# A two-layer stream encoder on one core: 40 hidden chunks ahead of the second dense stage, and its gates in three passes of 4, 5 and 7 blocks

## The chip, the core and the metric

The kernel runs on one core of a Trainium2 chip. The metric is the device time of one execution in microseconds (us). Engine names are those of the profile: PE is TensorE, PEld its weight loads, DVE VectorE, ACT ScalarE, POOL GpSimd, SP SyncE. POOL and SP only issue DMAs here: POOL the gathers by index (q0), SP the rest (q1).

## What is computed

Two layers run over 512 new frames (four blocks B0 to B3 of 128 tokens) and a sample of 64 tokens (S). Each layer has a mixer (attention, mLSTM, chunk MLP) and then PEER, a layer of 16384 one-neuron experts of which each token uses 8 heads x 16:

```python
def block(xi):                       # peer(), shortened
    q = (xi @ w_q)...                # 8 heads, normalised
    s = jnp.einsum('thcd,hckd->thck', q, keys)
    ...                              # top 16 of 128 x 128 per head: experts e, softmax gates g
    act = jax.nn.gelu(jnp.einsum('thkd,td->thk', u_tab[e], xi), approximate=False)
    return jnp.einsum('thk,thkd->td', (g * act), v_tab[e])
x = x + peer(xn2, peer_wq, peer_keys, peer_u, peer_v)
```

u_tab and v_tab are 16384 x 1024 floats each. A final RMSNorm follows.

## The kernel before

PEER is done in two ways at the same time. For two of the four blocks (256 tokens; B2 and B3 in layer 1) it is **dense**: all 16384 experts are gone through in 128 chunks of 128 experts. The other tokens are **gathered**: for each of a token's pairs POOL fetches the row of u or v by index, one row for each of 128 tokens, 512 KB. DVE multiplies a u row with the normalised input and sums it (L984), and adds a v row, times its gated activation, to the token's x (L996). In layer 1 blocks B0 and B1 are gathered beside the dense stage: 128 u tiles, then 128 v tiles, for B0 and then for B1, 512 in all. The 64 pairs of S are done earlier.

The dense stage of a layer (`peer_dense`, `first_gate`, `gate_batch`) works so, chunk by chunk:
- A **lead** loads the U chunk (SP, 512 KB, two buffers) and PE makes the hidden values H of 256 tokens, 8 products of 256 columns (L1059, in the trace 16 entries, since a float32 product has two). ACT applies the gelu into a tile `pre` or `A` (L1068). The first 8 x PRE chunks go to `pre`, whole blocks of 8 chunks that take gate buffers; later ones go to single tiles `A`, LAG + 2 of them.
- DVE multiplies the hidden chunk with its gates (L1092), in place.
- The V chunk is loaded (SP, two buffers) and PE adds the chunk's **product** to the outputs y, 4 products of 512 columns (L1099, 8 entries).

The **gates** are a matrix of 256 tokens x 16384 experts, nearly all zero. It is built in 16 blocks W of 8 chunks. A **pass** builds the blocks of one span at once, in 32 **batches** of 8 tokens. In each batch DVE makes a one-hot `o2` of 1024 elements per partition (L1020), a one-hot `o1` whose width goes with the blocks of the span (L1022), and weights it (L1024, twice that width). PE multiplies them, 16 weight loads and 16 products as wide as 8 x the blocks (L1028), and ACT copies the result into each block (L1030). QB lists the blocks of each pass. Before, layer 1 has two passes of 8. The first pass (`first_gate`) stands ahead of chunk 0; the others stand among the chunks of the span before, in its last WIN chunks:

```python
left = ci - (nq - win) + 1
while more and left > 0 and done < min(32, left * 32 // (win - 1)):
    if not nxt:
        nxt = [self.gate_block(l, c // 8 - ci // 8 + nb + i) for i in range(QB[l][q + 1])]
    self.gate_batch(nxt, c - ci + nq, 8 * done, self.psum([8, 8 * len(nxt)]))
    done += 1
if nl < NCH and len(acts) <= lag:
    lead(nl)
```

So a lead is issued only while no more than LAG (8) hidden chunks are in hand: after 8 x PRE + LAG leads ahead, the first 8 x PRE chunks have none of their own. HOME gives each block's buffer: `0` one tile of its own, `a` one of GATE_A = 4, which `pre` shares, `b` one of GATE_B[1] = 5. A buffer is waited for until its last reader is done.

A scheduler orders each engine's instructions when the program is built; gathers have low priority and fill DVE's gaps, but once ordered, each engine keeps to its order. Gate products are tied behind the last gate batch issued (`behind`). The final norm of a token block (`final`) squares on ACT (L236) into one tile `y` that all share, so each waits for the output DMA of the one ahead.

Of the kernel before, what the change touches and what calls it, by code (L numbers as in the profile page):

```python
# [36 lines left out]
WT = 1056  # L37
TD = 256
NG = TD + NS
QB = [[8, 8], [8, 8]]  # L40
WIN = [[24], [16]]
GATE_A, GATE_B = 4, [6, 5]
HOME = ["0aaabbbbbba0aaab", "0aabbbbbaa0aabbb"]
MID = 10 ** 6
LOW = 10 ** 7
PS_TAG = {"p": "mm", "a": "mm", "r": "mm", "o": "o", "tp": "tr", "ta": "tr", "tr": "tr"}
# [2 lines left out]
T_BUFS = {"t": 4, "tr": 2}  # L49
DENSE_T = 4  # L50
LAG = [4, 8]
PRE = [1, 2]
EARLY_LEADS = 5
REST_STEP, REST_PARTS = 4, 16
ORDER = ["N1 P1 N2 Q1 M1+P2 O1+Q2 S1+M2 F1+O2 S2", "N1 P1 Q1 M1+R O1 S1 N2 P2 F1+Q2 M2 O2"]
# [65 lines left out]
class Build:  # L121
# [911 lines left out]
    def gate_block(self, l, b):  # L1033
        home = HOME[l][b]
        pool, tag = (self.ca, "W0") if home == "0" else (self.wb if home == "a" else self.wb2, "W")
        W = pool.tile([P, 8, TD], F32, tag=tag, name=tag)
        return W

    def first_gate(self, l):
        nb = QB[l][0]  # L1040
        self.W0 = [self.gate_block(l, i) for i in range(nb)]
        for t0 in range(0, TD, 8):
            self.gate_batch(self.W0, 0, t0, self.psum([8, 8 * nb]))
            if l == 0:
                self.gated = self.mark.ins
            yield

    def peer_dense(self, l, group, xT):
# [5 lines left out]
        def lead(c):  # L1054
            U = self.up.tile([P, KC, P], F32, tag="U", name="U")
            nc.sync.dma_start(U, h["uT"][l, c])
            hp = hh[:, c % 2]
            for k in range(KC):
                mm = nc.tensor.matmul(hp, U[:, k, :], xT[k], start=(k == 0), stop=(k == KC - 1))  # L1059
                if k == 0 and l and c < 8 * PRE[l] + lag:  # L1060
                    self.behind(mm, self.smark.ins)
            if c < 8 * PRE[l]:
                if c % 8 == 0:
                    pre.append(self.wb.tile([P, 8, TD], F32, tag="W", name="pre"))
                a = pre[-1][:, c % 8, :]
            else:
                a = self.da.tile([P, TD], F32, tag="A", name="A", bufs=lag + 2)
            nc.scalar.activation(a, hp, AF.Gelu)  # L1068
            acts.append(a)
        for c in range(8 * PRE[l] + lag):  # L1070
            lead(c)
# [3 lines left out]
        Ws = self.W0  # L1075
        for q, nb in enumerate(QB[l]):
            more = q + 1 < len(QB[l])
            nxt, done = [], 0
            nq = 8 * nb
            win = WIN[l][q] if more else 0  # L1080
            for ci in range(nq):
# [5 lines that stand above are left out]
# [30 lines left out]
    def run(self):  # L1117
# [9 lines left out]
        for l in range(DEPTH):  # L1127
# [20 lines left out]
            with ExitStack() as es:  # L1148
                self.dense_pools(es.enter_context, l)
                nlead = LAG[l] + 8 * PRE[l]  # L1150
                if l == 0:
# [115 lines left out]
```

## Time and profile before

| what | us |
|---|---|
| median of three runs | 3598.27 (3591.49 to 3602.72) |
| the profiled execution | 3593.99 |
| its span, first to last instruction | 3592.2 |
| PE busy in it | 3078.9 (86%) |
| DVE busy | 2568.6 (72%) |
| ACT busy | 669.8 (19%) |
| mean DMA rate | 295 GB/s |

Busy shares are means over stages with different limits; the table of stretches below is read by stage. Queues on one engine run in order, so an instruction that waits holds up all that stands behind it. "Chunk" below is always one of the 128 chunks of layer 1's dense stage.

### The profile page before, as it was taken

The page shows a single profiled execution, that of the slowest core. Times are in us where ns is not written, and L with a number is a line of the kernel's source. Part 1 is how long each engine was busy: PE and PEld are TensorE (multiplying, and loading weights), DVE is VectorE, ACT ScalarE, POOL GpSimd, SP SyncE. Part 2 cuts the span into 40 slices and gives each one's busy share as a digit, 9 for nine tenths or more (in the row PEclk, how much of TensorE's full clock was granted, in tenths as well). Part 3 has the DMA queues.
Part 4 walks back from the last instruction along what each step waited for, and adds up shares of the span by engine and source line. Part 5 has one row for each costly group of instructions (what it writes and reads, how often), then busy time and mean ns, then how long its engine had stood idle before and what let it go on. Part 6 is the DMA issues. An engine that isn't in the chain of part 4 may idle for free.

```text
span 3592.2 us, 41429 instructions
## 1 busy us (share of the span) xinstructions
PE 3078.9 (86%) x13384; PEld 2057.7 (57%) x13384; DVE 2568.6 (72%) x5915; ACT 669.8 (19%) x2589; POOL 1540.9 (43%) x1284
## 2 busy tenths in 40 slices
PE   8989877789999999996977896589636999999996
PEld 6767646646666666653543654267512666666663
DVE  4454777776787666667688898847997679666664
ACT  4444222400121000001221222122210012000000
POOL 0000000065545445547657335610777666565562
PEclk9999989889999999998978997699858999999998
DMA  5332322289999999999979687853989999999995
GB/s 182 101 98 82 95 91 86 80 327 409 386 341 392 409 407 398 409 409 376 352 225 349 237 317 276 287 192 114 339 290 380 409 386 358 404 397 393 407 400 214
DMA packets 299929, 1060.21 MB, mean 295 GB/s; under 512 B 36372, under 2 KB 39232, under 8 KB 299712
## 3 DMA queue, kind: packets, MB, share of 16 engines
q0 software_dynamic: 184320, 671.17, 49.7%
q1 hardware_dynamic: 115392, 386.38, 29.9%
q8 instruction: 107, 1.75, 0.2%
q14 instruction: 110, 0.90, 0.1%
HBM read 1048.09 MB, written 8.27 MB: 294 GB/s over the span
## 4 chain that ended last, share of the span: by engine, by line
PE 44%; DVE 17%; DMA 16%; issue 14%; POOL 7%; ACT 2%; SPq 0%; POOLq 0%; DVEq 0%; ACTq 0%
PE H L1059 12%; PE y L1099 11%; DMA row<-in_peer_v_dram,idx 10%; PE ps L396 7%; POOL row L960 7%; PE ps L407 6%; DVE row L984 4%; DMA row<-in_peer_u_dram,idx 3%; DVE x_b L996 2%; PE ps L216 1%; PE ps L1028 1%; PE ps L572 1%; PE ps L830 1%; PE ps L574 1%; DVE o L1020 1%
## 5 line engine op out<-in xcount | busy, mean ns | idle before, releaser
L960 POOL DMA_INDIRECT row<-in_peer_u_dram,idx x640 | 776.6, 1213 | 1456.4 <-DVE row L984 822.4
L960 POOL DMA_INDIRECT row<-in_peer_v_dram,idx x640 | 764.1, 1194 | 542.4 <-DVE x_b L996 277.6
L984 DVE SCALAR_TENSOR_TENSOR row<-row,xn 128x1024 f32<-128x1024 f32 x640 | 769.8, 1221 | 178.1 <-DMA row<-in_peer_u_dram,idx 169.0
L1099 PE MATMUL y<-V,A 128*128 128x512 f32 x1856 | 845.4, 604 | 32.2 <-DMA V<-in_peer_v_dram 32.0
L996 DVE SCALAR_TENSOR_TENSOR x_b<-row,hb,x_b 128x1024 f32<-128x1024 f32 x512 | 656.2, 1282 | 158.5 <-DMA row<-in_peer_v_dram,idx 150.0
L1099 PEld LDWEIGHTS y<-V,A 128*128 128x128 f32 x1856 | 356.2, 194 | 421.5 <-issue 398.5
L1059 PE MATMUL H<-xT,U 128*128 128x256 f32 x2048 | 475.3, 385 | 35.2 <-ACT A L1068 20.4
L1059 PE MATMUL H<-xTd,U 128*128 128x256 f32 x2048 | 468.5, 382 | 10.2 <-ACT A L1068 8.2
L1059 PEld LDWEIGHTS H<-xT,U 128*128 128x128 f32 x2048 | 384.5, 191 | 125.8 <-ACT A L1068 39.4
L1059 PEld LDWEIGHTS H<-xTd,U 128*128 128x128 f32 x2048 | 386.7, 191 | 103.9 <-issue 40.4
L407 PE MATMUL ps<-xT,w 128*128 128x320 f32 (+1 forms) x1280 | 336.4, 417 | 28.3 <-DMA w<-in_wt_dram 17.2
L1068 ACT ACTIVATE A<-H 128x256 f32<-128x256 f32 x232 | 88.9, 383 | 1346.2 <-PE H L1059 751.2
L407 PEld LDWEIGHTS ps<-xT,w 128*128 128x128 f32 x1280 | 244.3, 195 | 95.4 <-issue 13.3
L1092 DVE TENSOR_TENSOR A<-A,W 128x256 f32<-128x256 f32 x232 | 96.8, 422 | 217.5 <-ACT A L1068 209.6
L1030 ACT ACTIVATE W<-ps 128x64 f32<-128x64 f32 x1024 | 137.8, 321 | 295.7 <-PE ps L1028 202.7
L1028 PE MATMUL ps<-o,o 128*128 128x64 f16 x2048 | 85.9, 199 | 119.6 <-DVE o L1024 119.6
L996 DVE SCALAR_TENSOR_TENSOR x_s<-row,hb,x_s 128x1024 f32<-128x1024 f32 x128 | 164.1, 1282 | 32.9 <-DMA row<-in_peer_v_dram,idx 31.1
L1028 PEld LDWEIGHTS <-o 128*128 128x128 f16 x2048 | 79.9, 102 | 151.5 <-DVE o L1024 75.4
L1099 PE MATMUL y<-V,pre 128*128 128x512 f32 x192 | 105.0, 704 | 38.9 <-DMA V<-in_peer_v_dram 31.1
L396 PE MATMUL ps<-w,xT 128*128 128x512 f32 (+3 forms) x320 | 128.9, 554 | 5.7 <-DMA w<-in_wn_dram 5.7
L351 DVE TENSOR_TENSOR wl<-w,wh 128x1024 fp32r<-128x1024 f32 (+1 forms) x56 | 64.4, 1150 | 75.9 <-PE ps L396 56.0
L396 PE MATMUL ps<-w,mix 128*128 128x512 f32 (+1 forms) x224 | 110.9, 648 | 5.8 <-DMA w<-in_wn_dram 4.2
(314 smaller groups left out, 3004.6 us busy)
## 6 DMA issues: line engine op xcount, KB each, us to landing
V<-in_peer_v_dram SPq DMA_DIRECT2D x256, 512.0 KB
U<-in_uT_dram SPq DMA_DIRECT2D x256, 512.0 KB
w<-in_wt_dram SPq DMA_DIRECT2D x96, 512.0 KB
w<-in_wn_dram SPq DMA_DIRECT2D x80, 512.0 KB
row<-in_peer_u_dram,idx POOLq DMA_INDIRECT x640
row<-in_peer_v_dram,idx POOLq DMA_INDIRECT x640
w<-in_keysT_dram SPq DMA_DIRECT2D x16, 256.0 KB
w<-in_wn_dram SPq DMA_DIRECT2D x8, 264.0 KB
```

Source lines behind the costliest of these rows:

```text
L351: self.nc.vector.tensor_tensor(lo, src, hi.bitcast(F32), op=ALU.subtract)
L396: self.nc.tensor.matmul(p[:t.n, :wd], x[kk][:, t.c0:t.c0 + t.n], ww[:, k * wd:(k + 1) * wd], start=(kk + part + j == 0), stop=(kk == KC - ...
L407: self.nc.tensor.matmul(ps, ww[:, k * P:(k + 1) * P], x[k][:, :n], start=(k + part + j == 0), stop=(k == KC - 1 and part == pair and j == ...
L960: self.nc.gpsimd.indirect_dma_start(out=row, out_offset=None, in_=self.h[tab], in_offset=bass.IndirectOffsetOnAxis(ap=t.idx[:, k:k + 1], a ...
L984: nc.vector.scalar_tensor_tensor(row, row, 1.0, xn, op0=ALU.mult, op1=ALU.mult, accum_out=hb[:, k:k + 1])
L996: op = nc.vector.scalar_tensor_tensor(x, row, t.hb[:, k:k + 1], x, op0=ALU.mult, op1=ALU.add)
L1028: nc.tensor.matmul(pb[:, j, :nq], o2[:, j // 2, :, j % 2], o1[:, p, j // 2, :, j % 2], start=(p == 0), stop=(p == 1))
L1030: nc.scalar.activation(W[:, :, t0:t0 + 8].rearrange("p i t -> p t i"), pb[:, :, 8 * i:8 * i + 8], AF.Copy, scale=1.0 / GSCALE)
L1059: mm = nc.tensor.matmul(hp, U[:, k, :], xT[k], start=(k == 0), stop=(k == KC - 1))
L1068: nc.scalar.activation(a, hp, AF.Gelu)
L1092: gated = nc.vector.tensor_tensor(a, a, Ws[ci // 8][:, ci % 8, :], op=ALU.mult)
L1099: nc.tensor.matmul(ys[i][:, hf, :], a[:, i * P:(i + 1) * P], V[:, hf * 512:(hf + 1) * 512], start=(c == 0), stop=(c == NCH - 1))
```

## The change

Only constants of layer 1 (the second entry of each list) differ. PRE goes from 2 to 4, so 32 + 8 leads are planned ahead instead of 16 + 8. QB goes from passes of 8 and 8 blocks to 4, 5 and 7. WIN places the second pass in the last 16 of the first 32 chunks and the third in the last 24 of the next 40. HOME moves the blocks: `pre` fills all four `a` buffers at first, so the first pass uses `0` and three `b`.

```diff
-QB = [[8, 8], [8, 8]]
-WIN = [[24], [16]]
+QB = [[8, 8], [4, 5, 7]]
+WIN = [[24], [16, 24]]
 GATE_A, GATE_B = 4, [6, 5]
-HOME = ["0aaabbbbbba0aaab", "0aabbbbbaa0aabbb"]
+HOME = ["0aaabbbbbba0aaab", "0bbbbbaa0aabbbbb"]
...
 LAG = [4, 8]
-PRE = [1, 2]
+PRE = [1, 4]
```

POOL's order is the same in both. The others are the same up to the start of layer 1's first pass.

ACT in the first pass. W is a gate block, `pre` a hidden chunk of a lead. Before, the later part of the pass:

```order
L987 ACTIVATE hb<-hb 128x32
L1068 ACTIVATE A<-H 128x256
L1030 ACTIVATE W_15775<-ps 128x8x8
L1030 ACTIVATE W<-ps 128x8x8 x7
L1030 ACTIVATE W_15775<-ps 128x8x8
L1030 ACTIVATE W<-ps 128x8x8 x7
```

and after:

```order
L1068 ACTIVATE pre<-H 128x256
L1030 ACTIVATE W_15953<-ps 128x8x8
L1030 ACTIVATE W<-ps 128x8x8 x3
L1030 ACTIVATE W_15953<-ps 128x8x8
L1030 ACTIVATE W<-ps 128x8x8 x3
L1068 ACTIVATE pre<-H 128x256
```

Before, no lead follows once the one shown is done, and the pass goes on alone; after, a lead stands behind every two batches to its end, and a batch has four copies instead of eight. On PE 27 leads stand ahead of chunk 0's product before and 33 after; leads 34 to 43 follow among the products of chunks 2 to 11, and the next, number 44, among those of chunk 34.

DVE in the second pass of the kernel after, which before has no counterpart at these chunks (there the gate products of chunks 0 to 25 stand in one piece behind the first pass). `row<-row,xn` is a gathered u row, `x_b` a v row, `pre<-pre,W` a chunk's gate product:

```order
L1020 TENSOR_TENSOR o_17151<-jj,sel 128x1024
L1022 TENSOR_TENSOR o_17152<-jj,sel 128x4x80
L1020 TENSOR_TENSOR o_17178<-jj,sel 128x1024
L1022 TENSOR_TENSOR o_17179<-jj,sel 128x4x80
L984 SCALAR_TENSOR_TENSOR row,hb<-row,xn 128x1024
L1024 TENSOR_TENSOR o_17152<-o_17152,sel 128x8x80
L984 SCALAR_TENSOR_TENSOR row,hb<-row,xn 128x1024
L1024 TENSOR_TENSOR o_17179<-o_17179,sel 128x8x80
L1092 TENSOR_TENSOR pre<-pre,W 128x256
```

The gate products of chunks 18 to 31 are now spread among 26 batches and 43 gathers, about two of each per chunk late in the pass. Counted over DVE's order, 92 gathers and 34 batches stand ahead of chunk 0's gate product before, 59 and 34 after; ahead of chunk 18's, 118 gathers after; ahead of chunk 31's, 161.

DVE at the end of the program, before:

```order
L1092 TENSOR_TENSOR A<-A,W 128x256
L996 SCALAR_TENSOR_TENSOR x_b_75<-row,hb,x_b_75 128x1024 x3
L1092 TENSOR_TENSOR A<-A,W 128x256
L996 SCALAR_TENSOR_TENSOR x_b_75<-row,hb,x_b_75 128x1024 x13
L226 TENSOR_SCALAR rs_v<-ss 128x1
```

and after:

```order
L1092 TENSOR_TENSOR A<-A,W 128x256
L996 SCALAR_TENSOR_TENSOR x_b_75<-row,hb,x_b_75 128x1024 x33
L1106 TENSOR_TENSOR x_b_80<-y_14714,x_b_80 128x1024
L996 SCALAR_TENSOR_TENSOR x_b_75<-row,hb,x_b_75 128x1024
L1106 TENSOR_TENSOR x_b_82<-y_14715,x_b_82 128x1024
L996 SCALAR_TENSOR_TENSOR x_b_75<-row,hb,x_b_75 128x1024 x11
L226 TENSOR_SCALAR rs_v<-ss 128x1
```

Behind the last gate product 13 gathers are left before and 45 after, and the dense outputs (L1106) are now added among them. In between, both have 3 or 4 gathers per chunk.

## Rows read from the trace of the kernel before

**Rows 1.** The page: the rate in 40 slices, and the queues.
```profile
GB/s 182 101 98 82 95 91 86 80 327 409 386 341 392 409 407 398 409 409 376 352 225 349 237 317 276 287 192 114 339 290 380 409 386 358 404 397 393 407 400 214
DMA packets 299929, 1060.21 MB, mean 295 GB/s; under 512 B 36372, under 2 KB 39232, under 8 KB 299712
...
q0 software_dynamic: 184320, 671.17, 49.7%
q1 hardware_dynamic: 115392, 386.38, 29.9%
```

**Rows 2.** Stretches: start:end, length, then busy us by engine, clock, DMA.
```profile
2510.00:2580.00 70.00, 54.44 (x429) 44.98 (x428) 65.61 (x121) 20.81 (x133) 47.70 (x35) 0.96 0.93 332
2580.00:2677.00 97.00, 19.68 (x299) 16.78 (x297) 92.25 (x165) 18.68 (x137) 77.78 (x55) 0.54 0.89 307
2677.00:2776.00 99.00, 69.07 (x160) 28.60 (x161) 78.68 (x138) 3.54 (x16) 63.77 (x52) 0.85 0.94 355
2776.00:2930.00 154.00, 148.79 (x509) 95.36 (x508) 106.86 (x99) 9.59 (x30) 95.66 (x79) 1.00 1.02 404
2930.00:3060.00 130.00, 129.53 (x857) 88.14 (x856) 114.81 (x174) 37.49 (x252) 81.73 (x58) 1.00 0.98 362
3060.00:3530.00 470.00, 452.81 (x1545) 290.61 (x1544) 306.30 (x428) 27.53 (x73) 277.54 (x226) 1.00 1.01 398
3530.00:3592.00 62.00, 37.58 (x72) 14.65 (x70) 23.09 (x48) 3.44 (x6) 5.35 (x5) 0.80 0.42 147
```

**Rows 3.** PE in order of time: leads 17 and 27 (start, us, what).
```profile
2516.10 3.72 PE L1059 MATMUL H<-xT,U 128*128 128x256 f32 x16 [0.47 <-ACT pre L1068]
...
2577.39 2.90 PE L1059 MATMUL H<-xT,U 128*128 128x256 f32 x6 [2.23 <-DMA U<-in_uT_dram]
```

**Rows 4.** DVE: the first two gathers, and the first gate products.
```profile
2510.54 1.22 DVE L984 SCALAR_TENSOR_TENSOR row<-row,xn 128x1024 f32<-128x1024 f32 x1
...
2511.68 1.22 DVE L984 SCALAR_TENSOR_TENSOR row<-row,xn 128x1024 f32<-128x1024 f32 x1
...
2677.19 5.45 DVE L1092 TENSOR_TENSOR pre<-pre,W 128x256 f32<-128x256 f32 x16
```

**Rows 5.** DVE in the second pass, one after the other without a gap.
```profile
2965.14 0.42 DVE L1092 TENSOR_TENSOR A<-A,W 128x256 f32<-128x256 f32 x1
2965.48 0.68 DVE L1020 TENSOR_TENSOR o<-jj,sel 128x1024 f16<-128x1024 f16 x1
2966.09 0.42 DVE L1022 TENSOR_TENSOR o<-jj,sel 128x512 f16<-128x512 f16 x1
2966.42 1.28 DVE L996 SCALAR_TENSOR_TENSOR x_b<-row,hb,x_b 128x1024 f32<-128x1024 f32 x1
2967.62 0.68 DVE L1024 TENSOR_TENSOR o<-o,sel 128x1024 f16<-128x1024 f16 x1
2968.22 1.28 DVE L996 SCALAR_TENSOR_TENSOR x_b<-row,hb,x_b 128x1024 f32<-128x1024 f32 x1
```

**Rows 6.** PE: products of chunk 0 (its first entries) and of chunk 16.
```profile
2677.67 2.93 PE L1099 MATMUL y<-V,pre 128*128 128x512 f32 x3 [3.54 <-DVE pre L1092]
...
2776.36 3.60 PE L1099 MATMUL y<-V,A 128*128 128x512 f32 x8
```

**Rows 7.** PE: two gate batches between two leads, and chunk 52.
```profile
2972.53 1.12 PE L1028 MATMUL ps<-o,o 128*128 128x64 f16 x32
2973.49 3.70 PE L1059 MATMUL H<-xT,U 128*128 128x256 f32 x16
...
3044.30 3.68 PE L1099 MATMUL y<-V,A 128*128 128x512 f32 x8
```

**Rows 8.** PE: chunk 119, the first without a lead ahead of it.
```profile
3529.52 5.37 PE L1099 MATMUL y<-V,A 128*128 128x512 f32 x8 [2.03 <-DMA V<-in_peer_v_dram]
```

**Rows 9.** DVE: last gate product and last gather; ACT: the last two final norms.
```profile
3524.51 0.42 DVE L1092 TENSOR_TENSOR A<-A,W 128x256 f32<-128x256 f32 x1 [3.37 <-ACT A L1068]
...
3545.11 1.29 DVE L996 SCALAR_TENSOR_TENSOR x_b<-row,hb,x_b 128x1024 f32<-128x1024 f32 x1 [1.22 <-DMA row<-in_peer_v_dram,idx]
...
3576.19 1.06 ACT L236 ACTIVATE y<-x_b 128x1024 f32<-128x1024 f32 x1 [28.56 <-DVE x_b L1106]
...
3583.93 1.06 ACT L236 ACTIVATE y<-x_b 128x1024 f32<-128x1024 f32 x1 [6.59 <-DMA out_dram<-y]
```

## The prediction

> **What bounds the kernel now.** I read the page first, then the stretches of layer 1, then single rows of TensorE (PE) and VectorE (DVE) in them. The change touches nothing ahead of the last stage of layer 1, so only the time from the first routed gather there (2510.5 us, [rows 4]) to the end at 3592.2 us is at stake.
>
> Over the whole program the DMA engines move 1060 MB, most of it gathered rows on q0, and reach 409 GB/s in their best slices [rows 1]. One gathered row tile, one U chunk and one V chunk are 512 KB each, so 1.28 us of that rate. From 2510 us on there are 512 gathers and nearly all of the 256 U and V chunks to move. At 1.28 us each the DMA has some 960 us of work for the 1035 us up to the last gather, 3545.1 us [rows 9]. The limits change by stretch [rows 2]:
> - 2510 to 2677: the first gate pass. DVE is full (92 of 97 us in its second part), PE is nearly empty (20 of 97 us) at a granted clock of 0.54, and the DMA moves only 307 GB/s.
> - 2677 to 2776: chunks 0 to 15, V products alone, since their 16 hidden blocks were computed ahead. 98.7 us [rows 6], 6.17 us per chunk, set by V loads that share the DMA with gathers.
> - 2776 to 3530: each chunk has a lead (H, 8 products) and its V product (y). PE is full. y of chunk 52 starts at 3044.3 and that of chunk 119 at 3529.5 [rows 7, 8]: 485 us for 67 chunks, 7.24 us each. The DMA moves 398 to 404 GB/s beside it, so PE and DMA are both near their limits.
> - 2930 to 3060: the same with the second gate pass in it. PE 129.5 of 130 us, DVE 115.
> - after 3530: PE's last chunks, then final norms.
>
> So the waste is ahead of 2677: PE has nothing to do, because only 24 leads were planned ahead (27 stand there in the built order) and everything else waits for all 8 gate blocks.
>
> **Part 1: 4 gate blocks in the first pass.** Per batch DVE runs three instructions, 1024, 512 and 1024 elements wide: 0.61 + 0.33 + 0.60 = 1.54 us from start to start [rows 5]. Only the last two depend on the width. Half the width by the line through these points (0.27 us per 512 elements) gives 0.61 + 0.20 + 0.33 = 1.14 us. In DVE's order 92 gathers and 34 batches stand ahead of chunk 0 before, 59 and 34 after. A u gather is 1.145 us on DVE [rows 4]. Before: 92 x 1.145 + 34 x 1.54 = 158 us against 166.7 measured from 2510.5 to 2677.2 [rows 4], 5.7% over. After: 59 x 1.145 + 34 x 1.14 = 106 us, with the same 5.7% 112 us. Chunk 0 at 2623. If the narrower forms gained nothing, it would be 14 us more; that no such form is in the trace makes this the bound on that side. On the other side nothing below 0.61 us per batch can go, since the 1024-wide one-hot is unchanged.
>
> **Part 2: 16 more leads.** Leads number 17 and 27 start at 2516.1 and 2577.4 [rows 3], 6.13 us per lead with gathers beside. Now 33 leads stand ahead of chunk 0 in PE's order: the 33rd starts at 2516.1 + 16 x 6.13 = 2614 and ends by 2618, inside the 2623. So these 6 cost nothing: DVE's own 112 us hide them. If that cover went (the first pass were shorter), they would end the stage five us sooner and no more. Each lead also brings a U load, which the DMA has room for at 307 GB/s, and a gelu on ACT, which is busy for 19 of 97 us there [rows 2]. On SP the loads of U 33 to 35 now stand ahead of chunk 2's V, and SP waits for a free U buffer; that is inside the 7.24 us below. The other 10 (34 to 43) stand between V products of chunks 2 to 11. I give those 12 chunks the steady 7.24 us, and chunks 12 to 17 the 6.17 us of V alone: 87 + 37 = 124 us. DVE's gathers meanwhile, 59 up to chunk 18, take 114 us at the 51 per 98.7 us that the order and [rows 6] give for the V stretch before. Chunk 18 at 2747.
>
> **Part 3: a second pass of 5 blocks, inside a stretch with no leads.** It runs from chunk 18 to 31 and DVE sets it: 10 u gathers, 33 v gathers at 1.20 us, 26 batches at 0.61 + 0.23 + 0.40 = 1.24 us, 13 gate products at 0.34 us [rows 5]: 11.5 + 39.6 + 32.2 + 4.4 = 88 us, with 5.7% 93. PE's own work there, 13 x 3.6 [rows 6] + 26 x 0.48 = 59 us, hides behind it. The pass adds a wait: blocks 6 and 7 go into buffers of `pre`, so ACT's copies wait until chunk 15's product has read them, and behind them stand only more copies, since the next lead is number 44. No one waits for ACT then before chunk 32, so it costs nothing unless the pass starts ahead of chunk 16; it does by 3 batches, which the products of those chunks on PE don't wait for. Chunk 32 at 2747 + 93 + 1 = 2841. Before, 14 chunks with their leads took 14 x 7.24 = 101 us, so 14 leads' worth of PE time comes back only in small part here, because DVE now sets the pace; and the DMA is slack (57 loads, 73 us).
>
> **Part 4: a third pass of 7 blocks.** This is 32 batches more work than before. DVE has 0.61 + 0.30 + 0.54 = 1.45 us for one and still has room under PE: per chunk 3.4 x 1.20 + 2.1 x 1.45 + 0.34 = 7.5 us, about PE's. PE has 16 weight loads and 16 products per batch. Two batches push the next lead from 2972.53 to 2973.49, so 0.48 us each at 64 columns [rows 7]. From chunk 32 to 52 there are 2 chunks without a lead, 18 with one and 30 batches: 2 x 3.6 + 18 x 7.24 + 30 x 0.48 = 152 us. Chunk 52 at 2993 instead of 3044, 51 us earlier.
>
> How far the price of a batch follows its width is not in the trace: all rows are 64 columns. At the one end three passes (32 + 40 + 56 columns) cost PE what two of 64 did, and the 14 us fall away; at the other each batch costs 0.48 us whatever its width. I take the upper end, since with 128-column weight loads as many as products the row is nearer to it. The Trainium skill ("TensorE: Matmul & The Clock Gate", section "Wait — 56ns, not 53.3ns?") says that products never start less than about 25 ns apart however narrow they are. That speaks against splitting a pass. By it a narrow batch is at least 16 x 25 = 400 ns (an estimate from the page), and the 30 batches cost 12 us rather than 0 or 14. The row has 30 ns per product at 64 columns, which agrees; no run so far shows a narrower one.
>
> **Part 5: the end.** Chunks 52 to 119 keep their 7.24 us: 485 us, so chunk 119 at 3478. But the gathers are tied to DVE's order, 3.5 per chunk, and start this stretch 33 behind: 45 stand after the last gate product instead of 13. That product is 5 us ahead of chunk 119's y (3524.5 against 3529.5, [rows 8, 9]), so 3473. Then 45 gathers and 8 V chunks at 1.28 us are 68 us; 45 at the 1.58 us that the 13 took before (20.6 us) are 71. Last gather at 3541. Three final norms now follow it, where before PE's last chunk had two after it: the first starts when the last accumulation ends (1.3 us), each further one 7.74 us later, and the last needs 8.3 us to the end [rows 9]: 1.3 + 15.5 + 8.3 = 25 us. End at 3566. So half of the 51 us is given back: gathers become what ends last, not PE.
>
> The profiled run lasted 3594.0 us (span 3592.2 and 1.8 around it), 4.3 under the median of 3598.3. The gain is 26 us, 0.7%: **3572 us** on the median.
>
> **Rivals.**
> 1. The leads that stand between V products are not hidden at all. PE takes H and y in order, and U and V have two buffers each. If a chunk then costs a U period and a product, 6.13 + 3.6 = 9.7 us instead of 7.24, ten of them cost 25 us, and the gain is 1 us: 3597, the same. For it: V alone takes 6.17 us per chunk, well over the 3.6 of its product [rows 6]. Against: in the steady stretch U and V together keep to 7.24 us with the DMA just as full.
> 2. The second pass goes in lock step, and the kernel gets slower. A batch has two buffers for its one-hots; DVE may build the next only after PE's products, which stand behind a y that waits for the gate product that stands behind the batch on DVE. Then a chunk costs the sum, 93/13 = 7.2 on DVE plus 3.6 + 1.0 on PE, 11.8 us, and 13 chunks 60 us more: 3632. From 9.2 us per chunk on the gain is gone. For it: the order has two batches, then a gate product, again and again. Against: in the pass of before, with the same buffers, PE and DVE were both nearly full [rows 2].
> 3. More is won: narrow batches are cheap on PE (14 us) and the DMA fills up beside the second pass, so that fewer gathers are left at the end: some 20 us more, 3552 or a little below.
> 4. Nothing is really moved, because the scheduler set its own order: excluded, the order has 33 leads ahead of chunk 0 for 27.
>
> **How the numbers follow.** 0.3% is 11 us, about what a measurement of this kernel can tell from no change. The forecast with its own spread, 3557 to 3587 (14 us for the first pass and as much for batches on PE), has 0.55; rival 1 and milder forms of it, 3588 to 3608, 0.21; rival 2 with anything over 3609, 0.14; rival 3 0.10. Faster 0.65, same 0.21, slower 0.14. The range is 3548 to 3604.
>
> **What would show it.** In the profile of the changed kernel: chunk 0 of layer 1 at about 2623 and PE busy and at full clock ahead of it; chunk 18 at 2747; DVE full to about 2841 and the DMA slack; chunk 52 at 2993; 7.24 us per chunk after that; the last gather after the last V product, and 25 us from it to the end. If chunk 52 comes later than some 3019, the gain is lost. If the 45 last gathers take less than 60 us, I was too low on the gain.

## The result, and the profile after

| | median us | range | runs |
|---|---|---|---|
| before | 3597.34 | 3591.49 to 3602.72 | 4 |
| after | 3565.58 | 3560.13 to 3575.88 | 4 |

The ratio is 0.9919 (95% interval 0.989 to 0.9947), a gain of 0.8%, or 32 us by the medians. Measured once more in a later group, ten runs beside 16 of the kernel before, it was 0.9953 (0.9937 to 0.9969). So the gain is 0.5 to 0.8% by the two ratios, 0.3 to 1.1% by their intervals, and the direction is not in doubt.

The profiled execution of the kernel after lasted 3575.88 us, the slowest of its four. Its last stage begins at 2519.95 us, 9.4 us later than before, by differences ahead of the change. All comparisons of traces below therefore count from the first gather of the stage. The stretches of the kernel after (start:end, length, then busy us by engine, clock, DMA, as in [rows 2]):

```profile
2519.00:2629.00 110.00, 89.86 (x806) 74.56 (x805) 106.34 (x219) 26.26 (x147) 82.17 (x59) 0.92 0.95 353
2629.00:2740.00 111.00, 98.77 (x375) 59.53 (x375) 77.96 (x142) 7.39 (x32) 67.03 (x55) 0.95 0.99 386
2740.00:2850.00 110.00, 79.15 (x579) 39.77 (x578) 106.00 (x188) 22.12 (x149) 74.48 (x51) 0.89 0.90 322
2850.00:3000.00 150.00, 145.57 (x922) 97.19 (x921) 132.73 (x175) 33.52 (x216) 85.84 (x69) 1.00 0.98 372
3000.00:3472.00 472.00, 464.96 (x1636) 307.33 (x1633) 318.26 (x456) 30.99 (x96) 229.14 (x230) 0.99 1.02 404
3472.00:3550.00 78.00, 35.87 (x74) 14.18 (x72) 65.35 (x54) 0.38 (x1) 52.97 (x46) 0.80 0.96 369
3550.00:3574.00 24.00, 0.00 (x0) 0.00 (x0) 10.12 (x37) 3.45 (x6) 0.00 (x0) 0.50 0.16 66
```

In the first pass DVE is still full (106 of 110 us), and PE now works beside it: 90 of 110 us at a granted clock of 0.92, where [rows 2] had 20 of 97 at 0.54 in its later part. The second pass (third row) belongs to DVE, 106 of 110 us, and the DMA is slack at 322 GB/s. Then PE is nearly full for 622 us, and in the last hundred us it is mostly DVE and the DMA that work.

DVE's milestones: the first gather, the first gate products, the last gate product, the last gather.

```profile
2519.95 1.22 DVE L984 SCALAR_TENSOR_TENSOR row<-row,xn 128x1024 f32<-128x1024 f32 x1
...
2628.90 2.43 DVE L1092 TENSOR_TENSOR pre<-pre,W 128x256 f32<-128x256 f32 x7
...
3478.89 0.42 DVE L1092 TENSOR_TENSOR A<-A,W 128x256 f32<-128x256 f32 x1
...
3549.75 1.29 DVE L996 SCALAR_TENSOR_TENSOR x_b<-row,hb,x_b 128x1024 f32<-128x1024 f32 x1 [0.67 <-DMA row<-in_peer_v_dram,idx]
```

PE's: the products of chunks 16, 32, 119 (with 120) and 127.

```profile
2739.42 3.68 PE L1099 MATMUL y<-V,pre 128*128 128x512 f32 x8
...
2849.34 3.68 PE L1099 MATMUL y<-V,A 128*128 128x512 f32 x8
...
3472.11 7.18 PE L1099 MATMUL y<-V,A 128*128 128x512 f32 x16
...
3515.87 5.09 PE L1099 MATMUL y<-V,A 128*128 128x512 f32 x8 [2.99 <-DMA V<-in_peer_v_dram]
```

ACT's squares of the three final norms behind the last gather:

```profile
3551.12 1.06 ACT L236 ACTIVATE y<-x_b 128x1024 f32<-128x1024 f32 x1 [78.42 <-DVE x_b L996]
...
3558.47 1.06 ACT L236 ACTIVATE y<-x_b 128x1024 f32<-128x1024 f32 x1 [6.20 <-DMA out_dram<-y]
...
3565.84 1.06 ACT L236 ACTIVATE y<-x_b 128x1024 f32<-128x1024 f32 x1 [6.22 <-DMA out_dram<-y]
```

In one table, us from the first gather of the stage, each read from single rows of the trace like these:

| | before | after | passes only (two traces) |
|---|---|---|---|
| chunk 0, gate product | 167 | 109 | 116, 116 |
| chunk 16, product | 266 | 219 | 212, 211 |
| chunk 32 | 378 | 329 | 338, 337 |
| chunk 52 | 534 | 480 | 492, 492 |
| chunk 119 | 1019 | 952 | 971, 970 |
| chunk 127, PE's last | 1062 | 996 | 1023, 1018 |
| last gather | 1035 | 1030 | 1031, 1028 |
| end | 1082 | 1054 | 1055, 1053 |

The table has the main story. PE's last chunk comes 66 us earlier, the last gather 5 us earlier. The end is whichever comes later: 19 us from the start of PE's last chunk, two norms included (before: 1062 + 19), or 24 us from the last gather, three norms included (after: 1030 + 24). So 28 us of the 66 are seen, and the third column, which lacks the 16 early leads, sees the same. The last gather has little room to move: from the first one on the DMA moves 394 MB in both kernels, an estimated 963 us at the 409 GB/s of its best slices [rows 1].

### The profile page after: what moved, and what is told of

Same layout as the page of the kernel before. It is cut to its first block, busy times and chain, and to the rows that moved or that the text cites. A ratio compares the mean times of both kernels' runs of the same rounds, so it can differ in the third digit from the quotient of the medians.

```text
span 3574.1 us, 42595 instructions
## 1 busy us (share of the span) xinstructions
PE 3095.6 (87%) x13896; PEld 2082.1 (58%) x13896; DVE 2598.3 (73%) x6011; ACT 672.9 (19%) x2589; POOL 1497.6 (42%) x1284
## 4 chain that ended last, share of the span: by engine, by line
PE 34%; DMA 18%; DVE 17%; issue 17%; POOL 11%; ACT 2%; POOLq 0%; SPq 0%; another core or an unknown queue 0%; DVEq 0%; ACTq 0%
POOL row L960 11%; DMA row<-in_peer_v_dram,idx 10%; PE ps L396 7%; PE H L1059 7%; PE ps L407 7%; PE y L1099 5%; DMA row<-in_peer_u_dram,idx 5%; DVE row L984 4%; DVE x_b L996 3%; PE ps L216 1%; PE ps L572 1%; DMA V<-in_peer_v_dram 1%; PE ps L574 1%; DVE o L1020 1%; PE ps L830 1%
## 5 line engine op out<-in xcount | busy, mean ns | idle before, releaser
L960 POOL DMA_INDIRECT row<-in_peer_u_dram,idx x640 | 732.7, 1145 | 1505.2 <-DVE row L984 889.7
L1099 PE MATMUL y<-V,A 128*128 128x512 f32 x1728 | 792.6, 604 | 34.8 <-DMA V<-in_peer_v_dram 27.4
L1099 PEld LDWEIGHTS y<-V,A 128*128 128x128 f32 x1728 | 330.2, 193 | 378.6 <-issue 336.6
L1059 PEld LDWEIGHTS H<-xT,U 128*128 128x128 f32 x2048 | 393.9, 194 | 109.4 <-issue 41.2
L407 PE MATMUL ps<-xT,w 128*128 128x320 f32 (+1 forms) x1280 | 344.4, 424 | 23.7 <-DMA w<-in_wt_dram 17.0
L1099 PE MATMUL y<-V,pre 128*128 128x512 f32 x320 | 160.6, 651 | 19.6 <-DMA V<-in_peer_v_dram 16.8
L1028 PE MATMUL ps<-o,o 128*128 128x64 f16 (+3 forms) x2560 | 93.9, 187 | 89.2 <-DVE o L1024 85.7
L1028 PEld LDWEIGHTS <-o 128*128 128x128 f16 x2560 | 87.9, 98 | 134.3 <-DVE o L1024 61.0
L1020 DVE TENSOR_TENSOR o<-jj,sel 128x1024 f16<-128x1024 f16 x160 | 109.9, 688 | 41.7 <-PE ps L1028 40.4
L912 DVE MAX8 v<-s 128x8 f32<-128x128 f32 x128 | 32.9, 283 | 123.3 <-ACT s L833 123.2
```

The source lines that it names most:

```text
L407: self.nc.tensor.matmul(ps, ww[:, k * P:(k + 1) * P], x[k][:, :n], start=(k + part + j == 0), stop=(k == KC - 1 and part == pair and j == ...
L960: self.nc.gpsimd.indirect_dma_start(out=row, out_offset=None, in_=self.h[tab], in_offset=bass.IndirectOffsetOnAxis(ap=t.idx[:, k:k + 1], a ...
L1020: nc.vector.tensor_tensor(o2, self.jj[:, None].to_broadcast([P, 4, P, 2]), sel[:, 1, :, None, :].to_broadcast([P, 4, P, 2]), op=ALU.is_equal)
L1028: nc.tensor.matmul(pb[:, j, :nq], o2[:, j // 2, :, j % 2], o1[:, p, j // 2, :, j % 2], start=(p == 0), stop=(p == 1))
L1099: nc.tensor.matmul(ys[i][:, hf, :], a[:, i * P:(i + 1) * P], V[:, hf * 512:(hf + 1) * 512], start=(c == 0), stop=(c == NCH - 1))
```

## The experiments

Three groups of runs, each beside its own runs of the kernel before, which took 3598.7, 3585.6 and 3583.3 us in the median. Since these differ, ratios are compared, and where an expectation has microseconds, the ratio times 3598 is set against it.

**The split of the passes alone**, run twice.

```diff
-PRE = [1, 4]
+PRE = [1, 2]
```

> Only the split of the gate passes (4, 5 and 7 blocks) is kept; 24 leads are planned ahead as before (27 stand ahead of chunk 0 in the built order, 33 in the changed kernel), and TensorE keeps its pairs of leads and products. My theory, that the shorter pass is of use only because leads fill TensorE while VectorE works: chunk 0 comes 109 to 112 us after the first gather as in the changed kernel, but the 16 leads not made early have to be made between products: 6 more leads among chunks 2 to 17 and 10 or more beside the second pass, at 1 to 3.6 us each, so chunk 52 comes some 25 to 30 us later than in the changed kernel, and the pace after it is 7.24 us per chunk as before, not 7.05. End at 3580 to 3595. Rival A, the split alone brings the gain: 3560 to 3570, the same as the changed kernel.

> The split of the passes alone (24 leads planned ahead), once more. Theory now: gathers end last in both, 1030 us after the first one, so the 16 leads more are worth nothing that reaches the end: the same as the changed kernel within 0.3%. Rival, the leads carry a good part of the gain and the first comparison missed it: slower than the changed kernel by 0.4% or more.

Measured 0.9924 (0.9896 to 0.9953), and the second time 0.993 (0.9905 to 0.9956), beside 0.9953 for the full change in the same group. Those two intervals overlap, within the 0.3% expected the second time, and the split alone has the lower ratio. My first expectation was 3580 to 3595; 0.9924 is 3571. That expectation falls. The table above says why: without the leads chunk 52 is 12 us later, PE's last chunk 22 to 27 us later, and neither reaches the end, because the gathers and their norms end 12 to 16 us after PE and its two norms. (For chunk 52, 25 to 30 us had been expected. But chunks 18 to 32, which have 14 leads here and none after, took 108 us for 90, so only 1.3 us per lead.) The first gather, PE's last two chunks, and the last gather of the second of these runs:

```profile
2501.81 1.22 DVE L984 SCALAR_TENSOR_TENSOR row<-row,xn 128x1024 f32<-128x1024 f32 x1
...
3514.40 8.80 PE L1099 MATMUL y<-V,A 128*128 128x512 f32 x16 [3.39 <-DMA V<-in_peer_v_dram]
...
3530.17 1.28 DVE L996 SCALAR_TENSOR_TENSOR x_b<-row,hb,x_b 128x1024 f32<-128x1024 f32 x1
```

> The changed kernel once more, beside the next one on the same chip, so that the two are compared directly. 0.9919 of the kernel before had been measured; expected 0.989 to 0.995.

Measured 0.9953, as said.

**32 early leads for 40.**

```diff
-PRE = [1, 4]
+PRE = [1, 3]
```

> The changed kernel with 32 H chunks planned ahead in layer 1 for 40; the gate passes of 4, 5 and 7 blocks stay, and TensorE alternates one lead and one product as in the changed kernel. My theory: chunk 0 at the same 109 us after the first gather, since VectorE sets it; 8 leads more fall between later products, where each costs 1 to 3.6 us of TensorE time, partly hidden beside the second pass, so chunk 52 is 8 to 20 us later than in the changed kernel; the gathers, which set the end there, give about half of it back: 3569 to 3580. If the number of leads were of no account (rival A): 3562 to 3568. If the lead count alone did it, half of the gain is gone: 3581.

Measured 0.989 (0.9858 to 0.9923), 3557 us: not slower than 40 at all, so that this expectation falls too. Its chunk 52 is at 480 us, as with 40, where 8 to 20 us more had been expected. So 24, 32 and 40 leads give 0.9924 and 0.993, 0.989, 0.9919 and 0.9953: no trend that the intervals bear out. The traces hint that 40 are too many: with 32 the last gather is at 1014 us for 1030, and with the other ending below at 1023 for 1036. From 220 to 330 us after the first gather, beside the second pass, the DMA moves 387 and 353 GB/s there, with 40 leads 322 and 316. The other half of the change by itself, 40 leads with two passes of 8, was not tried: `pre` would take all four `a` buffers, and 8 blocks don't go into one `0` and five `b`.

**The order on PE alone.** In the kernel after, PE alternates one lead and one product; before, and with the passes alone, it does two and two. Nobody wrote that; the scheduler did. Put into the kernel before:

```diff
                 if k == 0 and l and c < 8 * PRE[l] + lag:
                     self.behind(mm, self.smark.ins)
+                elif k == 0 and l and last:
+                    self.behind(mm, last[0])
```

(`last` holds the y product issued last.)

> The kernel before with one change of order on TensorE alone: each later lead's first product is put behind the last y product issued, so that leads and products alternate one by one instead of two by two. Passes, lead count and all work are those of the kernel before. In the changed kernel this alternation came about by itself, and the steady stretch went at 7.05 us per chunk for 7.24. If that is the order's doing (theory), the 67 chunks from 52 to 119 take 472 us for 485 here too, and, since TensorE's chunks end last in this kernel, 10 to 13 us of it reach the end: 3584 to 3588. If the whole gain of the changed kernel were this by-product (rival B): 3565 to 3570. If the pace in the changed kernel comes from somewhere else (gathers that lag and so compete less for the DMA): no change, 3594 to 3600.

Measured 0.9997 (0.9972 to 1.0022). What PE waits for in chunks 64 to 96, before, after and here (engine and line, what it waited for: us in total, times, longest):

```profile
PE H L1059 <- ACT A L1068: 7.6, 16, 0.5
```
```profile
PE H L1059 <- ACT A L1068: 0.3, 1, 0.3
```
```profile
PE y L1101 <- DVE x_b L996: 2.3, 1, 2.3
PE H L1059 <- DMA U<-in_uT_dram: 0.3, 1, 0.3
```

The second of two leads in a row waits 0.47 us for a gelu, once per two chunks. Alternation takes that away: these 32 chunks took 232 us before, 221 after and 225 here (4 of them the wait of 2.3 us and the slow product behind it), that is 7.26, 6.90 and 7.03 us each, and the passes-only kernel, which has pairs, again took 232. So the mechanism is as expected, and it explains the faster steady stretch of the kernel after. But no gain shows in the time, to within some 10 us: the same rule left only 24 leads and put 101 gathers ahead of chunk 0 instead of 92, PE was 12 us late by chunk 52, and the last lead waited 8.5 us for a gelu. In the profiled execution alone the stage ended 8 us sooner than before (1073 us for 1082), which the ratio of the twelve runs doesn't confirm. That the changed order is the whole gain is out.

**The other ending**, on both kernels. The norm squares into a scratch tile and writes in place, so it needn't wait for the output DMA of the norm ahead, and only B1's norm stands behind the last gather.

```diff
-        y = self.ca.tile([P, DM], F32, tag="xn", name="y", bufs=1)
-        r = self.rstd(self.sumsq(x[:n], n, y[:n]), n, 1, 1.0 / DM)
+        junk = self.sm.tile([P, DM], BF16, tag="junk", name="junk", bufs=1)
+        r = self.rstd(self.sumsq(x[:n], n, junk[:n]), n, 1, 1.0 / DM)
+        y = x
...
-        for t in [S] + B:
+        for t in [S, B[0], B[2], B[3], B[1]]:
```

> The changed kernel with another ending: the final norm of a block writes in place and squares into a scratch tile of its own, so that one block's norm needn't wait until the output of the one before has left, and the norms go in the order S, B0, B2, B3, B1, so that only B1's stands behind the last gather. Theory: gathers end last in the changed kernel, not TensorE (last V product at 3516 to 3520, last gather at 3550, end at 3574 in the trace), so the two norms of 7.4 us each that are taken from behind the last gather come off the end: 3549 to 3553, 13 to 16 us under the changed kernel. Rival C, TensorE still sets the end: no change against the changed kernel, 3563 to 3568.

> The kernel before with the other ending (norm in place, squares into a scratch tile, order S, B0, B2, B3, B1), which brought the changed kernel about 10 us. Theory: here two norms must follow TensorE's last V product in any order, and the last gather is 27 us ahead of it, so only the wait for the output of the norm before goes: 0 to 6 us, 3592 to 3599. If the ending were worth the same wherever TensorE stands: 3588.

After: 0.9892 (0.9869 to 0.9915), 10 us under the kernel after as first measured (those two intervals overlap) and 22 under its second measurement. Before: 0.9986 (0.997 to 1.0002), most likely 5 us, in the expected 0 to 6. ACT's squares in the changed kernel with this ending, whose last gather is at 3538.74:

```profile
3515.93 1.06 ACT L236 ACTIVATE junk<-x_b 128x1024 bf16<-128x1024 f32 x1 [58.47 <-DVE x_b L1106]
...
3518.30 1.06 ACT L236 ACTIVATE junk<-x_b 128x1024 bf16<-128x1024 f32 x1 [1.22 <-DVE rs_v L226]
...
3540.12 1.06 ACT L236 ACTIVATE junk<-x_b 128x1024 bf16<-128x1024 f32 x1 [20.67 <-DVE x_b L996]
```

B2's and B3's norms are done well ahead of the last gather, and from it to the end are 9.7 us instead of 24.4. The 10 us are under the 13 to 16 expected; in this trace the last gather itself came 6 us later (1036). That PE sets the end of the kernel after is out.

**Half of layer 1's v rows not fetched**, in three kernels.

```diff
-            row = self.gather(t, "peer_v", k)
+            if not (t.lay and t.blk is not None and k % 2):
+                row = self.gather(t, "peer_v", k)
```

> The kernel before, where in layer 1 every second v row of the 128-token blocks isn't fetched (VectorE uses the row before it once more), so the output differs. 128 of the 512 gathers of the last stage fall away, 64 MB or 164 us of DMA at 1.28 us each; VectorE, TensorE and all orders keep their work. Theory: in the kernel before TensorE sets the end (7.24 us per chunk, its last V product 17 us after the last gather's end), so this frees the DMA for nothing: 3582 to 3598. Rival, the DMA sets the end here too: 3530 to 3570.

> The changed kernel with the same half of layer 1's v rows left out (output differs). Theory: there the gathers end last, and the steady stretch at 7.05 us per chunk is set by the DMA (404 to 409 GB/s). With 128 transfers less the chunks go at 6.7 to 6.9 us (15 to 20 us less from chunk 52 to 119), the gathers behind the last gate product take VectorE's 1.28 us each, 58 us for 71, and the end comes 25 to 50 us earlier: 3515 to 3540. Rival C, TensorE sets the end in the changed kernel as before: 3555 to 3566.

> The split of the passes alone (24 leads), with half of layer 1's v rows left out (output differs). With the gathers off the end, the TensorE time that 16 early leads save must show: in the traces TensorE's last V product came 27 us later without them (1023 against 996 us after the first gather). Theory: 12 to 27 us behind the changed kernel with the same rows left out, so 0.9765 to 0.981 of the kernel before, for 0.9731 there. Rival, the leads save TensorE nothing in itself: 0.973.

| v rows halved in | ratio | chunk 52 | PE's last chunk | last gather | end |
|---|---|---|---|---|---|
| before | 0.9869 (0.9843 to 0.9894) | 485 | 1008 | 861 | 1027 |
| passes only | 0.9795 (0.9764 to 0.9826) | 447 | 978 | 876 | 998 |
| after | 0.9731 (0.9705 to 0.9757) | 439 | 969 | 908 | 988 |

The last gathers and the last two chunks of PE, the kernel before first, then the changed kernel, then passes only:

```profile
3364.56 1.28 DVE L998 SCALAR_TENSOR_TENSOR x_b<-row,hb,x_b 128x1024 f32<-128x1024 f32 x1
...
3507.61 7.03 PE L1101 MATMUL y<-V,A 128*128 128x512 f32 x16
```
```profile
3431.81 3.92 DVE L998 SCALAR_TENSOR_TENSOR x_b<-row,hb,x_b 128x1024 f32<-128x1024 f32 x3
...
3492.07 7.03 PE L1101 MATMUL y<-V,A 128*128 128x512 f32 x16
```
```profile
3368.81 2.60 DVE L998 SCALAR_TENSOR_TENSOR x_b<-row,hb,x_b 128x1024 f32<-128x1024 f32 x2
...
3468.56 7.03 PE L1101 MATMUL y<-V,A 128*128 128x512 f32 x16
```

Two of three expectations missed. Before gained 47 us by its ratio where I had 0 to 16: 3551 us, inside the range of the rival by which the DMA sets the end, although in the trace PE ends last. And after gained 97 us against the kernel before, so 68 more than the change alone, where I had 25 to 50. One reason is that the edit did more than I wrote: the scheduler, with fewer transfers, put all gathers ahead of chunk 119's gate product, and PE alternates for most of the stage in all three. How much of the 47 us is the DMA's and how much the order's stays open; but among each other the three are alike, and they can be compared. With the gathers off the end, PE ends last in all three, and the full change is worth 39 us in the traces (1027 against 988), 44 by the medians (3537.7 and 3493.5) and 50 by the ratios, instead of 28. And here the leads show: without them the end is 9 us later in the traces, 23 us (0.0064) by the ratios; 12 to 27 had been expected. The ratios come from two groups, between which the kernel after itself differed by 0.0034. PE alternates in both of these kernels, so the 9 us are the leads' own; the 22 to 27 us by which PE's last chunk differs with all rows fetched hold the alternation too. In both pairs of kernels the leads save PE time; it reaches the end only where PE ends last.

One stretch of the first kernel is clean against the kernel before, since the order up to chunk 16 is the same: these 16 chunks took 85 us for 98.7 [rows 6], so they are limited by the DMA, as the prediction had it. And its last 39 chunks before number 119, with the DMA at only 276 GB/s, went at 6.89 us each: that is PE's own pace.

**The best version.**

> 32 H chunks planned ahead, passes of 4, 5 and 7 blocks, and the other ending. Theory: the number of early leads is slack (24, 32 and 40 gave 3574, 3557 and 3566 us, within their spread), the ending is worth about 10 us where gathers end last, so this comes out as the changed kernel with the other ending or somewhat under it: 3543 to 3558. If 32 leads were really better than 40 by 8 us and the ending adds its 7 to 10 us in full: 3545 to 3549. If both were chance: 3559 to 3566.

> 24 leads, passes 4, 5, 7, the other ending, and the second gate pass begun at chunk 4 of the first span instead of chunk 16 (window of 28 chunks for 16). In the changed kernel VectorE is full in the second pass (106 of 110 us) and the DMA slack there (322 GB/s), while in the stretch ahead VectorE has 33 us to spare. Theory: spread over more chunks, the batches leave room for gathers where the DMA was slack, and the last gather comes 5 to 15 us earlier than 1030 us after the first: 0.983 to 0.987 of the kernel before. Rival, the DMA is near its limit over the whole stage and nothing is to be had: as the changed kernel with the other ending, 0.9875 to 0.990.

32 leads with the other ending: 0.9876 (0.9854 to 0.9899), 3553 against the expected 3543 to 3558, and 43 us under the kernel before in its own group (3542.5 for 3585.6). It beats the kernel before and very likely the kernel after, but not certainly the one with 40 leads and the same ending (0.9892). Another version, with 24 leads, this ending and

```diff
-WIN = [[24], [16, 24]]
+WIN = [[24], [28, 24]]
```

spreads the second pass over 28 chunks: 0.99 (0.9874 to 0.9926) where 0.983 to 0.987 had been expected. Chunk 52 came 8 us earlier than with 24 leads and the old window (484 for 492), but the last gather stayed at 1032. The rival holds: what DVE can spare doesn't bring the gathers in sooner.

## Why the prediction came out right, and where it was wrong

**Part 1** held: chunk 0 at 109 us after the first gather for 112. The narrower forms take 0.28 and 0.42 us for 0.42 and 0.68, as the line through [rows 5] had it.

**Parts 2 and 3** held in time: chunk 32 at 329 us for 331, DVE full and the DMA slack in the second pass. Only the cover of the 33 leads was thinner than Part 2 had it: the last of them ended 1 us behind chunk 0's gate product instead of 5 us ahead. Rival 2, the lock step, didn't come: DVE waited 2.6 us for PE's gate products in the second pass and 5.7 in the third. Rival 1 didn't either: chunks 0 to 16 took 110 us with their ten leads, for 112 by the sums of Part 2.

**What they were credited with was wrong.** The prediction took PE's idle first pass for the waste and the leads for what fills it. The runs show that the split of the passes is enough (its three passes were not tested one by one). It lets chunk 0 start 50 us sooner without the leads and 58 with them, and the end that then binds, the gathers', is the same. The step that failed is one that was not taken: Part 5 found that gathers end last, but did not ask which parts of the change had still been needed to get there.

**Part 4**: chunk 52 at 480 for 483. The price of a batch is now in the trace. Two batches of 32 columns, two of 40, one of 56, each with PE's next start behind it, all at a granted clock of 1.00:

```profile
2568.23 0.95 PE L1028 MATMUL ps<-o,o 128*128 128x32 f16 x32
2569.03 3.27 PE L1059 MATMUL H<-xT,U 128*128 128x256 f32 x14
```
```profile
2800.76 0.96 PE L1028 MATMUL ps<-o,o 128*128 128x40 f16 x32
2801.56 3.68 PE L1099 MATMUL y<-V,pre 128*128 128x512 f32 x8
```
```profile
2905.16 0.58 PE L1028 MATMUL ps<-o,o 128*128 128x56 f16 x16 [1.22 <-DVE o L1024]
2905.58 3.68 PE L1099 MATMUL y<-V,A 128*128 128x512 f32 x8
```

That is 0.40, 0.40 and 0.42 us per batch for 0.48 at 64 columns [rows 7], or 25, 25, 26 and 30 ns per product. The 30 batches cost 13 us, not 14.4, so rival 3, cheap narrow batches, had little in it. From 40 to 32 columns nothing more is saved, which agrees with the Trainium skill ("TensorE: Matmul & The Clock Gate", section "Wait — 56ns, not 53.3ns?"), by which products start no closer than about 25 ns; by that figure the estimate had been 12.

**Part 5** had two errors that cancelled, which was luck. The pace was 7.05 us per chunk, not 7.24 (472 us for 67 chunks), so chunk 119 came at 952 us and not 968. The 7.24 was read as work of PE and DMA; 0.23 of it was the wait for the gelu (15.2 us in 32 waits over the 65 chunks of 3060 to 3530), which the alternation took away. Free of waits the kernel after goes at 6.90 us; its mean of 7.05 holds two waits (5.1 and 1.6 us) and a slow lead. On the other side the gate product of chunk 127 isn't 5 us ahead of chunk 119's product any more but 7 us behind it, since gate products stand among gathers on DVE and come at the gathers' pace. It was at 959 us for 962 expected. From there all held: 70.9 us for the 45 gathers (68 to 71), 24.4 us for three norms (25), the end at 1054 for 1056.

**"Half is given back"** held, and is now measured from both sides: 54 us at chunk 52 became 28 at the end; with half of the v rows not fetched the end keeps 39 to 50.

**"PE is full from 2776 on"** was too simple, and that the DMA was near its limit there did not hold PE. PE's own pace is 6.89 us per chunk with the DMA at 276 GB/s, and 6.90 in the kernel after (chunks 64 to 96) with the DMA at 409. In pairs it is 7.26, before and with the passes alone. So it was the order that held the steady stretch of the kernel before: from 3060 to 3530 us PE waited for a transfer only once, 2.0 us at chunk 119 [rows 8].

## What to carry to other kernels

Where two streams share a core and the program ends when both are done, work out both ends, each with what must follow it, before valuing a change to one: the gain is capped by the other, and each further edit to the first is worth nothing once it is under the cap, even if its saving is plain in the trace. Test the parts of a change singly even when the sum comes out right. And a busy share of 100% can hold a small wait in each period: look at the list of waits by stretch, not at the share.

## What the runs showed of the hardware

A short idle time on TensorE can cost more than itself, though it doesn't each time. In the kernel after, S's final norm, which shares a tile with the gathers of u and waited on ACT for the last of them, stood ahead of one gelu, and PE waited 5 us for that. ACT's rows, PE's, and the stretches from 3308 us on (granted clock is the third figure from the end):

```profile
3311.55 1.06 ACT L236 ACTIVATE y<-x_s 64x1024 f32<-64x1024 f32 x1 [13.44 <-DVE row L984]
...
3312.72 0.36 ACT L1068 ACTIVATE A<-H 128x256 f32<-128x256 f32 x1
```

```profile
3304.41 3.60 PE L1099 MATMUL y<-V,A 128*128 128x512 f32 x8
3313.13 5.78 PE L1059 MATMUL H<-xT,U 128*128 128x256 f32 x16 [5.13 <-ACT A L1068]
3318.76 3.60 PE L1099 MATMUL y<-V,A 128*128 128x512 f32 x8
```
```profile
3308.00:3313.00 5.00, 0.01 (x1) 0.00 (x0) 3.08 (x8) 1.45 (x4) 2.44 (x3) 0.75 1.03 410
3313.00:3316.00 3.00, 2.87 (x7) 2.34 (x8) 2.93 (x8) 0.08 (x1) 0.94 (x1) 0.50 1.00 392
3316.00:3319.00 3.00, 3.00 (x12) 2.50 (x11) 2.86 (x9) 0.04 (x1) 1.62 (x2) 0.78 0.92 296
3319.00:3322.00 3.00, 3.00 (x8) 1.33 (x7) 2.96 (x3) 0.34 (x1) 2.36 (x2) 1.00 0.79 247
```

Behind the idle time the clock is at 0.50, the lower of its levels (1.2 GHz), and the lead takes 5.78 us for 3.62: 2.2 us on top of the 5.1. The product of chunk 127 above (5.09 us behind 2.99 us of waiting) and chunk 119's of before (5.37 behind 2.03, [rows 8]) show the same, with a mean granted clock of 0.72 and 0.70. Chunk 121's product, in the same trace, doesn't: behind 3.08 us of waiting it took 3.67 us, all at a granted clock of 1.00. What tells these cases apart is not shown.

```profile
3482.37 3.67 PE L1099 MATMUL y<-V,A 128*128 128x512 f32 x8 [3.08 <-DMA V<-in_peer_v_dram]
```

The gathers' end hardly follows PE's: over the eleven traces with all rows fetched the last gather stood between 1014 and 1036 us, while PE's last chunk went from 990 to 1062.
